# A two-layer hybrid backbone: input loaded and normed first, turned vectors in one PSUM bank, context modulated last

## The chip, the cores and the metric

The kernel runs on one core of a Trainium2 chip. The metric is the device time of one execution in microseconds (us); of several runs the median is taken. One profiled execution gives the trace that is read here. In the trace PE is TensorE's matrix multiplication, PEld its weight load, DVE VectorE, ACT ScalarE, POOL GpSimd, and SP the engine whose queue issues most of the transfers (DMA) from memory.

## What is computed

Two layers work on a latent stream `x` of 512 tokens by 1024 channels; a context of 256 tokens takes part in the first one. Each layer norms its input, scales and shifts it by vectors that are products of a conditioning vector with a weight matrix, mixes tokens, and adds the gated result to the stream. Everything is float32. What matters here is the front of layer 0:

```
def _ada(cvec, w, b):
    m = jax.nn.silu(cvec) @ w + b
    return jnp.split(m, 3, axis=-1)          # shift, scale, gate

def _modulate(x, g, shift, scale):
    return _rmsnorm(x, g) * (1 + scale) + shift

...
shift, scale, gate = _ada(c, ada_w[i], ada_b[i])
h = _modulate(x, norm_g[i], shift[:, None], scale[:, None])
shift_c, scale_c, gate_c = _ada(c_ctx, ada_w[i], ada_b[i])
hc = _modulate(ctx, norm_g[i], shift_c, scale_c)
...
p = h @ w_in                                  # q, v, forward and backward forget, gate
```

Both `h` and `hc` are then multiplied by the same 1024 by 10240 matrix `w_in`, and a gated linear recurrence runs over the results, in 16 heads. Layer 1 is a convolution module. Neither the recurrence nor layer 1 is touched by the change.

## The kernel before

Channels lie on the 128 partitions, in eight blocks (`k` = 0 to 7); tokens run along the free dimension. Every float32 factor of a large product is split into two parts, `hi` (rounded by ScalarE) and `lo` (the remainder, by VectorE or GpSimd), and a product of `[128 x 128]` weights with 512 tokens is three matrix instructions: hi by hi, hi by lo, lo by hi.

The front of the program, inside the pool `pinit` (`pi`), has these pieces:

- The **conditioning products** come in four parts, `jj` = 0 to 3, each with four 512 KB tiles `ada`. `ada_start(jj)` multiplies them (L147, 16 instructions into the PSUM tile `adaps`), copies the result to SBUF (L149, `adarow`), turns it from a row into columns by four small products (L152, into a PSUM tile `adat`, a new one for each `jj`), and adds biases (L155, L156: `mod_s`, `mod_g`). `adaps`, `adat` and the sums of squares share the pool `ps_m`, which has two buffers under the tag `ms`.
- The **input** `x_sb` (2 MB, four loads) is squared and summed (`rms_rstd`: ACT L178, DVE or POOL L180, a product with ones at L186, then ACT L187 and L188). Part `jj` gives the scales of the channel blocks 2jj and 2jj+1: each is multiplied by the norm (L254, `xn`), scaled and shifted (`modulate`: ACT L192 writes `h_hi`, DVE L193 and L194 write `h_lo`).
- **Early products**: five weight pieces (`we`, 512 KB each; three in loop turn 0, two in turn 1) are loaded, split (L136, L138) and multiplied with each pair of blocks as soon as it stands (L243 to L245, PSUM tiles `pe`): 5 x 8 x 3 = 120 matrix instructions.
- The **context** `c_sb` (1 MB, two loads) is normed likewise (`rc`), multiplied by its norm on POOL (L266) and modulated into `hc`, tiles of 256 tokens. `CTX_AT` = 2 places its loads and norm in turn 2; `CTX_MOD` places six blocks of its modulation in turn 2 and two in turn 3.

Then `pinit` closes and the pool `pt` takes its memory. The first instructions that write into `pt` (ACT L580, which takes the finished early products out of PSUM into `sg`, and DVE L313) wait for the last use of the memory below them. The products with the context (`pc`, L293 to L296) follow on TensorE; they need a PSUM buffer that L580 frees. From there on eight groups of heads go through the recurrence.

Each engine executes its instructions in the order of its own queue. That order comes from a scheduler, which works with its own model of times when the kernel is built, except that the loads issued by `load` keep the order of the code among themselves. Tile names carry a running number in the listings below; `mod_s`, `mod_g`, `xn`, `h_lo`, `hc` and `c_sb` are as above.

Of the kernel before, what the change touches and what calls it, by code (L numbers as in the profile page):

```python
# [16 lines left out]
P = 128  # L17
# [18 lines left out]
EARLY, EARLY_LOADS, CTX_AT = 5, (3, 2, 0, 0), 2  # L36
RX_BUFS, RX_ENG, WE_ENG = 3, (0, 0, 1, 0, 0, 1, 0, 0), (1, 1, 0, 0, 0)
CTX_MOD = ((), (), (0, 1, 2, 3, 4, 5), (6, 7))
# [22 lines left out]
def hybrid_kernel(ctx: ExitStack, tc: tile.TileContext, xT, ctxT, cvec, consts, norm_g, ada_b, ada_a, ada_c,  # L61
# [79 lines left out]
    def ada_start(jj, raws, pool, scz, sel):  # L141

        ps = ps_m.tile([P, 512], F32, name=f"adaps{jj}", tag="ms")
        for kk, raw in enumerate(raws):
            for k in range(2):
                c = (2 * kk + k) % 4
                mm(ps[32 * c:32 * (c + 1)], lhsT=scz[:, 2 * kk + k, :], rhs=raw[:, k, :], start=(kk < 2), stop=(kk >= 2))  # L147
        row = pool.tile([P, 512], F32, name=f"adarow{jj}", tag="adarow", bufs=2)
        V.tensor_copy(out=row, in_=ps)  # L149
        pt_ = ps_m.tile([P, 512], F32, name=f"adat{jj}", tag="ms")  # L150
        for i in range(4):
            mm(pt_[:, 2 * i:2 * i + 2], lhsT=row[:, i * P:(i + 1) * P], rhs=sel, start=True, stop=True)  # L152
        for i in range(2):
            j = 2 * jj + i
            V.tensor_scalar(out=mod_s[:, j, :], in0=pt_[:, 2 * i:2 * i + 2], scalar1=ab[:, 0, j:j + 1], scalar2=None, op0=ALU.add)  # L155
            V.tensor_scalar(out=mod_g[:, j, :], in0=pt_[:, 4 + 2 * i:6 + 2 * i], scalar1=ab1[:, j:j + 1],  # L156
                            scalar2=ng[:, 0, j:j + 1], op0=ALU.add, op1=ALU.mult)

# [43 lines left out]
    with l0:  # L202
# [8 lines left out]
        with tc.tile_pool(name="pinit", bufs=1) as pi:  # L211
# [9 lines left out]
            for jj in range(4):  # L221
                araws.append([pi.tile([P, 2, 512], F32, name=f"ada{jj}_{kk}", tag="araw", bufs=8) for kk in range(4)])
                for kk in range(4):
                    load(araws[jj][kk], ada_a[jj, kk])
                if jj == 0:
                    for i in range(4):
                        load(x_sb[:, 2 * i:2 * i + 2, :], xT[:, 2 * i:2 * i + 2, :])
                for i in todo[:EARLY_LOADS[jj]]:
                    wraws.append(wpool.tile([P, KD, P], F32, name=f"we{i}_raw", tag="raw"))
                    load(wraws[i], wsrc[i])  # L230
# [7 lines left out]
            early, done = [], {}  # L238
# [9 lines left out]
            for jj in range(4):  # L248
                ada_start(jj, araws[jj], pi, scz, sel)
                if jj == 0:  # L250
                    rs = rms_rstd([x_sb[:, k, :] for k in range(KD)], L, pi, ps_m, "rx", RX_ENG)
                for k in (2 * jj, 2 * jj + 1):
# [715 lines left out]
```

## Time and profile before

| | |
|---|---|
| median of 3 runs | 1325.85 us (1321.75 to 1326.63) |
| the profiled execution | 1325.56 us, of which the span from the first to the last instruction is 1323.5 us |
| PE busy | 1288.8 us, 97% of the span |
| DVE, ACT, POOL busy | 934.4, 608.2, 304.3 us |
| chain that ended last, by engine | PE 77%, DVE 13%, ACT 4%, DMA 3%, waits for issue 2%, POOL 1% |
| mean granted TensorE clock | 0.991 |
| first product with the context | 69.89 us after the start |

TensorE is busy nearly throughout. The first of the page's 40 slices (33 us each) is the one in which it is least busy (6 tenths) and the transfers are most (9 tenths, 352 GB/s). The change touches only what lies ahead of 70 us.

### The profile page before, as it was taken

How to read it: one execution, taken by the hardware profiler on the slowest of the kernel's cores; microseconds unless marked ns; L12 is line 12 of the kernel's file. 1: busy time of each engine (PE TensorE's matmuls, PEld its weight loads, DVE VectorE, ACT ScalarE, POOL GpSimd, SP SyncE). 2: the span in 40 equal slices, each digit the busy share in tenths (PEclk: the TensorE clock that was granted, in tenths of full speed). 3: DMA queues.
4: the chain of work that ended last, by engine and by line, in shares of the span. 5: the costliest groups of instructions: out<-in, count | busy, mean ns of one | idle time of the engine just before them, and what ended most of it. 6: DMA issues, size and time to landing. Idle time of an engine off the chain costs nothing.

```text
span 1323.5 us, 19786 instructions
## 1 busy us (share of the span) xinstructions
PE 1288.8 (97%) x7956; PEld 1087.4 (82%) x7956; DVE 934.4 (71%) x1513; ACT 608.2 (46%) x920; POOL 304.3 (23%) x289
## 2 busy tenths in 40 slices
PE   6999999999999999999999999999999999999997
PEld 2698898888889888889889889876877778788887
DVE  6667987796787888687689788865666576574233
ACT  4355564552464354565256455524423233385331
POOL 2231330330231151151024033104212112112121
PEclk8999999999999999999999999999999999999999
DMA  9322113114112312213311311213433333123321
GB/s 352 156 80 79 51 49 128 49 49 159 54 47 77 128 49 77 84 49 97 112 36 62 122 39 48 75 48 108 135 103 122 120 96 119 64 80 96 96 80 64
DMA packets 36188, 120.22 MB, mean 91 GB/s; under 512 B 4643, under 2 KB 7107, under 8 KB 36097
## 3 DMA queue, kind: packets, MB, share of 16 engines
q1 hardware_dynamic: 35104, 115.79, 26.0%
q0 software_dynamic: 992, 3.18, 1.1%
q8 instruction: 62, 1.02, 0.3%
q14 instruction: 30, 0.24, 0.1%
HBM read 116.85 MB, written 2.10 MB: 90 GB/s over the span
## 4 chain that ended last, share of the span: by engine, by line
PE 77%; DVE 13%; ACT 4%; DMA 3%; issue 2%; POOL 1%; SPq 0%; DVEq 0%; ACTq 0%
PE pa L734 4%; PE pa L735 4%; PE pa L739 4%; PE pz L293 3%; PE pz L294 3%; PE pz L296 3%; PE op L563 2%; PE cop L876 2%; PE cop L880 2%; PE op L565 2%; PE op L564 2%; PE cop L877 2%; PE pgt L803 2%; PE pgt L801 2%; PE pgt L800 2%; PE py L773 2%
## 5 line engine op out<-in xcount | busy, mean ns | idle before, releaser
L734 PE MATMUL pa<-ci_hi,h_hi 128*128 128x512 f32 x256 | 100.3, 403 | 1.9 <-ACT h_hi L682 1.9
L735 PE MATMUL pa<-ci_lo,h_hi 128*128 128x512 f32 x256 | 99.7, 393 | 0.0
L293 PE MATMUL pz<-h_hi,wz_hi 128*128 128x512 f32 x232 | 92.1, 397 | 1.4 <-ACT wz_hi L136 1.4
L294 PE MATMUL pz<-h_lo,wz_hi 128*128 128x512 f32 x232 | 91.7, 395 | 0.0
L116 POOL TENSOR_SCALAR sg<-sg 128x1536 f32<-128x1536 f32 x16 | 75.6, 4726 | 63.6 <-ACT sg L582 63.3
L167 DVE SCALAR_TENSOR_TENSOR adacc<-adb,sc,adacc 128x128 f32<-128x128 f32 x224 | 76.9, 357 | 3.8
L424 DVE SCALAR_TENSOR_TENSOR h_S<-h_S,h_dec,h_kb 128x128 f32<-128x128 f32 x96 | 59.0, 614 | 27.1 <-ACT h_kb L418 26.0
L136 ACT ACTIVATE ci_hi<-ci_raw 128x1024 fp32r<-128x1024 f32 x29 | 30.8, 1061 | 102.2 <-PE pa L739 57.9
L138 POOL TENSOR_TENSOR ci_lo<-ci_raw,ci_hi 128x1024 fp32r<-128x1024 f32 x18 | 44.2, 2461 | 129.2 <-ACT ci_hi L136 102.9
L739 PE MATMUL pa<-ci_hi,h_lo 128*128 128x512 f32 x224 | 70.9, 392 | 0.0
L510 POOL TENSOR_TENSOR h_A<-a,a 128x512 f32<-128x512 f32 x16 | 36.6, 2290 | 129.8 <-DVE a L491 108.0
L304 PE MATMUL pv<-wv_hi,h_hi 128*128 128x256 f32 x256 | 63.3, 284 | 0.0
L305 PE MATMUL pv<-wv_hi,h_lo 128*128 128x256 f32 x256 | 63.3, 284 | 0.0
L296 PE MATMUL pz<-h_hi,wz_lo 128*128 128x512 f32 x232 | 60.7, 396 | 0.0
L734 PEld LDWEIGHTS pa<-ci_hi,h_hi 128*128 128x128 f32 x256 | 48.7, 190 | 14.1 <-issue 4.1
L136 ACT ACTIVATE wz_hi<-wz_raw 128x1024 fp32r<-128x1024 f32 x29 | 30.7, 1057 | 63.6 <-DMA wz_raw<-in_w_in 54.7
L294 PE MATMUL pc<-hc,wz_hi 128*128 128x256 f32 x232 | 59.1, 288 | 0.0
L293 PE MATMUL pc<-hc,wz_hi 128*128 128x256 f32 x232 | 58.8, 287 | 0.0
L735 PEld LDWEIGHTS pa<-ci_lo,h_hi 128*128 128x128 f32 x256 | 48.7, 190 | 11.5 <-issue 1.4
L138 DVE TENSOR_TENSOR wz_lo<-wz_raw,wz_hi 128x1024 fp32r<-128x1024 f32 x29 | 35.5, 1223 | 31.1 <-ACT wz_hi L136 30.7
L876 PE MATMUL cop<-zhi,co_hi 128*128 128x512 f32 (+1 forms) x160 | 54.2, 352 | 0.0
L369 POOL TENSOR_TENSOR h_ref<-h_tot,h_gt 128x64 f32<-128x64 f32 x16 | 16.8, 1048 | 160.5 <-DVE h_ref L396 157.3
(332 smaller groups left out, 3862.1 us busy)
## 6 DMA issues: line engine op xcount, KB each, us to landing
adb<-in_ada_c SPq DMA_DIRECT2D x32, 512.0 KB, 3.2
ci_raw<-in_c_in SPq DMA_DIRECT2D x32, 512.0 KB, 3.2
wz_raw<-in_w_in SPq DMA_DIRECT2D x29, 512.0 KB, 3.2
ada<-in_ada_a SPq DMA_DIRECT2D x16, 512.0 KB, 10.2
wv_raw<-in_w_v SPq DMA_DIRECT2D x16, 512.0 KB, 3.2
wg_raw<-in_w_in SPq DMA_DIRECT2D x16, 512.0 KB, 3.2
cg_raw<-in_c_gate SPq DMA_DIRECT2D x16, 512.0 KB, 3.2
co_raw<-in_c_out SPq DMA_DIRECT2D x16, 512.0 KB, 3.6
```

The costliest lines, as they stand in the source:

```text
L116: (G if pool_min else V).tensor_scalar(out=t, in0=t, scalar1=EMAX, scalar2=None, op0=ALU.min)
L138: lo_eng.tensor_tensor(out=lo, in0=raw, in1=hi.bitcast(F32), op=ALU.subtract)
L167: V.scalar_tensor_tensor(out=acc, in0=raw[:, k, :], scalar=sc[:, k, 0:1], in1=acc, op0=ALU.mult, op1=ALU.add)
L293: mm(ps[:, :T], lhsT=hi[:, k, :], rhs=rhi[k], start=(k == 0), stop=False)
L294: mm(ps[:, :T], lhsT=hi[:, k, :], rhs=rlo[k], start=False, stop=False)
L296: mm(ps[:, :T], lhsT=lo[:, k, :], rhs=rhi[k], start=False, stop=(k == KD - 1))
L304: mm(ps[:, :256], lhsT=lhi[k][:, c], rhs=hi[:, k % 4, :], start=(k == 0), stop=False)
L305: mm(ps[:, :256], lhsT=llo[k][:, c], rhs=hi[:, k % 4, :], start=False, stop=False)
L734: mm(pss[t], lhsT=h_hi[:, 2 * kq + k, c], rhs=hi[:, k, :], start=(kq == 0 and k == 0), stop=False)
L735: mm(pss[t], lhsT=h_hi[:, 2 * kq + k, c], rhs=lo[:, k, :], start=False, stop=False)
L739: mm(pss[t], lhsT=h_lo[:, 2 * kq + k, c], rhs=hi[:, k, :], start=False, stop=(kq == 3 and k == 1))
L876: mm(ps, lhsT=hi[:, i, c], rhs=zhi[ct][:, tok], start=(ct == 0), stop=False)
```

## The change

It does three things. The four loads of `x_sb` go ahead of the `ada` tiles of part 0, and the norm of the input (`rms_rstd`) stands ahead of `ada_start(0)` in the code. The turned vectors of all four parts go into one PSUM tile, `adat`, in the bank of the pool `ps_o`, each part with eight columns of it; the conditioning products of a part are issued after the last turning product of the part before. And the context is loaded and normed in turn 3 (`CTX_AT` = 3), with all eight blocks of its modulation there too.

```
-EARLY, EARLY_LOADS, CTX_AT = 5, (3, 2, 0, 0), 2
+EARLY, EARLY_LOADS, CTX_AT = 5, (3, 2, 0, 0), 3
-CTX_MOD = ((), (), (0, 1, 2, 3, 4, 5), (6, 7))
+CTX_MOD = ((), (), (), tuple(range(KD)))
...
-    def ada_start(jj, raws, pool, scz, sel):
+    def ada_start(jj, raws, pool, scz, sel, adat, last):
...
-                mm(ps[32 * c:32 * (c + 1)], lhsT=scz[:, 2 * kk + k, :], rhs=raw[:, k, :], start=(kk < 2), stop=(kk >= 2))
+                with tc.issue_after(last.ins) if last else nullcontext():
+                    mm(ps[32 * c:32 * (c + 1)], lhsT=scz[:, 2 * kk + k, :], rhs=raw[:, k, :], start=(kk < 2), stop=(kk >= 2))
...
-        pt_ = ps_m.tile([P, 512], F32, name=f"adat{jj}", tag="ms")
+        pt_ = cut(adat, 8 * jj, [[1, 8]])
         for i in range(4):
-            mm(pt_[:, 2 * i:2 * i + 2], lhsT=row[:, i * P:(i + 1) * P], rhs=sel, start=True, stop=True)
+            last = mm(pt_[:, 2 * i:2 * i + 2], lhsT=row[:, i * P:(i + 1) * P], rhs=sel, start=True, stop=True)
...
+        return last
...
-                for kk in range(4):
-                    load(araws[jj][kk], ada_a[jj, kk])
                 if jj == 0:
                     for i in range(4):
                         load(x_sb[:, 2 * i:2 * i + 2, :], xT[:, 2 * i:2 * i + 2, :])
+                for kk in range(4):
+                    load(araws[jj][kk], ada_a[jj, kk])
...
+            adat = ps_o.tile([P, 512], F32, name="adat", tag="o")
...
-                ada_start(jj, araws[jj], pi, scz, sel)
                 if jj == 0:
                     rs = rms_rstd([x_sb[:, k, :] for k in range(KD)], L, pi, ps_m, "rx", RX_ENG)
+                turned = ada_start(jj, araws[jj], pi, scz, sel, adat, turned)
```

The scheduler orders the queues anew, but only in this front part: behind it every engine's queue holds the same instructions in the same order. Three places show what moved (lines from L142 on stand one to three lower in the changed kernel).

VectorE at the first pair of channel blocks, before: the vectors of part 0 (`mod_s`, `mod_g`), then the rest of the input's squares, a weight split, and the multiplications by the norm.

```order
L149 COPY adarow_191<-adaps_182 128x512
L180 TENSOR_TENSOR rx_sq_202<-rx_sq_202,rx_sq_204 128x512
L155 TENSOR_SCALAR mod_s<-adat_193,ab 128x2
L156 TENSOR_SCALAR mod_g<-adat_193,ab_108,ng 128x2
...
L180 TENSOR_TENSOR rx_sq_202<-rx_sq_202,rx_sq_221 128x512
L138 TENSOR_TENSOR we_lo<-we_raw,we_hi 128x1024
L254 TENSOR_TENSOR xn_229<-x_sb,rx_sq_202 128x512
```

The same place now:

```order
L182 TENSOR_TENSOR rx_sq_183<-rx_sq_183,rx_sq_202 128x512
L257 TENSOR_TENSOR xn_229<-x_sb,rx_sq_183 128x512
...
L257 TENSOR_TENSOR xn_278<-x_sb,rx_sq_183 128x512
L150 COPY adarow_219<-adaps_210 128x512
L138 TENSOR_TENSOR we_lo<-we_raw,we_hi 128x1024
L156 TENSOR_SCALAR mod_s<-adat,ab 128x2
L157 TENSOR_SCALAR mod_g<-adat,ab_108,ng 128x2
```

The multiplications by the norm went ahead of the weight split, and the vectors of part 0 went behind it.

TensorE at the context's sum of squares (`rc_ss`), before: behind the turning of part 2 and ahead of the conditioning products of part 3.

```order
L245 MATMUL pe_293<-h_hi,we_lo 128x512
L152 MATMUL adat_335<-sel,adarow_333 128x2 x4
L186 MATMUL rc_ss<-rc_sq_384,ones 128x256
L147 MATMUL adaps_435<-ada_0_172,scz 32x512 x2
L147 MATMUL adaps_435<-ada_1_173,scz 32x512 x2
```

The same product now:

```order
L248 MATMUL pe_292<-h_hi,we_lo 128x512
L153 MATMUL adat<-sel,adarow_391 128x2 x4
L188 MATMUL rc_ss<-rc_sq_441,ones 128x256
L246 MATMUL pe_243<-h_hi,we_hi 128x512
L246 MATMUL pe_248<-h_hi,we_hi 128x512
```

It went behind the turning of part 3, the last one, and so behind 30 more early products; the conditioning products of part 3 (`adaps`) now stand ahead of all this.

VectorE at the last vectors (part 3) and the context, before: six blocks of the context stand ahead of `mod_s` and `mod_g` of part 3, two among the last blocks of the input.

```order
L193 TENSOR_SCALAR c_sb<-c_sb,mod_g,mod_s 128x256 x2
L194 TENSOR_TENSOR hc_114<-c_sb,hc_112 128x256
L155 TENSOR_SCALAR mod_s<-adat_446,ab 128x2
L156 TENSOR_SCALAR mod_g<-adat_446,ab_108,ng 128x2
L194 TENSOR_TENSOR hc_114<-c_sb,hc_112 128x256
...
L193 TENSOR_SCALAR xn_460<-xn_460,mod_g,mod_s 128x512
L193 TENSOR_SCALAR c_sb<-c_sb,mod_g,mod_s 128x256
L194 TENSOR_TENSOR h_lo<-xn_460,h_hi 128x512
L194 TENSOR_TENSOR hc_114<-c_sb,hc_112 128x256
L313 TENSOR_SCALAR qs_0_696<-pe_288 128x512
```

The same place now:

```order
L157 TENSOR_SCALAR mod_g<-adat,ab_108,ng 128x2
L195 TENSOR_SCALAR xn_401<-xn_401,mod_g,mod_s 128x512
L196 TENSOR_TENSOR h_lo<-xn_401,h_hi 128x512
L195 TENSOR_SCALAR xn_406<-xn_406,mod_g,mod_s 128x512
L196 TENSOR_TENSOR h_lo<-xn_406,h_hi 128x512
L195 TENSOR_SCALAR c_sb<-c_sb,mod_g,mod_s 128x256
L196 TENSOR_TENSOR hc_113<-c_sb,hc_111 128x256
...
L195 TENSOR_SCALAR c_sb<-c_sb,mod_g,mod_s 128x256 x2
L196 TENSOR_TENSOR hc_114<-c_sb,hc_112 128x256 x2
L316 TENSOR_SCALAR qs_0_693<-pe_287 128x512
```

All 16 context instructions of VectorE now stand behind the input's last block, directly ahead of the first instruction in the new pool. On the queue of SP the two context loads went from ahead of the `ada` tiles of part 3 to behind them, and two weight loads for later stages (`wz_11`, `wv_0`) went in among those tiles.

## Rows read from the trace of the kernel before

**Rows 1.** Windows: stretch in us, its length, each engine's busy us, PEclk, DMA share, GB/s.
```profile
24.00:46.00 22.00, 20.67 (x88) 12.42 (x89) 15.91 (x36) 8.25 (x16) 0.00 (x0) 1.00 0.98 378
...
58.00:60.00 2.00, 0.01 (x1) 0.01 (x1) 1.76 (x9) 0.88 (x2) 0.00 (x0) 1.00 0.00 0
60.00:69.20 9.20, 9.04 (x30) 6.64 (x30) 3.54 (x9) 1.63 (x3) 0.00 (x0) 0.81 0.01 2
...
70.00:110.00 40.00, 40.00 (x289) 37.88 (x290) 30.64 (x47) 25.43 (x38) 14.81 (x12) 1.00 0.24 80
```

**Rows 2.** Timeline to 34 us: start, us, engine, line, tiles [idle before <-releaser].
```profile
17.36 4.75 POOL L138 TENSOR_TENSOR we_lo<-we_raw,we_hi 128x1024 fp32r<-128x1024 f32 x2 [1.12 <-ACT we_hi L136]
...
18.77 1.06 ACT L136 ACTIVATE we_hi<-we_raw 128x1024 fp32r<-128x1024 f32 x1 [0.21 <-DMA we_raw<-in_w_in]
...
19.86 3.33 DVE L138 TENSOR_TENSOR we_lo<-we_raw,we_hi 128x1024 fp32r<-128x1024 f32 x1 [2.28 <-ACT we_hi L136]
...
21.84 0.63 ACT L188 ACTIVATE rx_sq<-rx_sq 128x512 f32<-128x512 f32 x1
...
23.12 2.48 DVE L254 TENSOR_TENSOR xn<-x_sb,rx_sq 128x512 f32<-128x512 f32 x4
...
23.84 1.52 ACT L192 ACTIVATE h_hi<-xn,mod_s,mod_g 128x512 fp32r<-128x512 f32 x2 [1.36 <-DVE xn L254]
...
27.28 0.50 PE L244 MATMUL pe<-h_lo,we_hi 128*128 128x512 f32 x1 [0.63 <-DVE h_lo L194]
...
33.89 1.34 ACT L178 ACTIVATE rc_sq<-c_sb 128x256 f32<-128x256 f32 x4
```

**Rows 3.** Chain that ended last, 41 to 48 us: start, us it adds, engine, line.
```profile
41.50 0.24 PE pe L244
41.74 0.98 PE adaps L147 x4
42.72 0.43 PE pe L244
...
46.39 0.80 PE adat L152 x8
```

**Rows 4.** Timeline from the turning of part 2 to the context's multiplication.
```profile
47.03 0.68 PE L186 MATMUL rc_ss<-rc_sq,ones 128*128 128x256 f32 x2
47.21 0.22 DVE L155 TENSOR_SCALAR mod_s<-adat,ab 128x2 f32<-128x2 f32 x1 [2.89 <-PE adat L152]
...
47.65 0.81 ACT L192 ACTIVATE h_hi<-xn,mod_s,mod_g 128x512 fp32r<-128x512 f32 x1 [8.86 <-DVE mod_g L156]
...
47.99 1.92 PE L147 MATMUL adaps<-ada,scz 128*32 128x512 f32 x16 [0.28 <-DVE mod_g L156]
...
49.44 0.41 ACT L188 ACTIVATE rc_sq<-rc_sq 128x256 f32<-128x256 f32 x1
...
49.92 7.05 POOL L266 TENSOR_TENSOR c_sb<-c_sb,rc_sq 128x256 f32<-128x256 f32 x8 [27.81 <-ACT rc_sq L188]
```

**Rows 5.** Timeline of the context's modulation and of the end of the front.
```profile
52.30 1.57 DVE L193 TENSOR_SCALAR c_sb<-c_sb,mod_g,mod_s 128x256 f32<-128x256 f32 x2
...
57.04 0.75 DVE L194 TENSOR_TENSOR hc<-c_sb,hc 128x256 fp32r<-128x256 f32 x2
...
59.12 0.81 ACT L192 ACTIVATE h_hi<-xn,mod_s,mod_g 128x512 fp32r<-128x512 f32 x1 [3.16 <-DVE mod_g L156]
...
69.24 1.58 ACT L580 ACTIVATE sg<-pe 128x512 f32<-128x512 f32 x3 [7.61 <-PE pe L245]
```

**Rows 6.** Lines L193 and L194, 45 to 70 us: times in ns, least/median/most.
```profile
L193 DVE TENSOR_SCALAR c_sb<-c_sb,mod_g,mod_s x8: 403/620/830, 52.3 to 62.2; 128x256 f32<-128x256 f32 x8
L193 DVE TENSOR_SCALAR xn<-xn,mod_g,mod_s x4: 542/545/547, 48.5 to 61.7; 128x512 f32<-128x512 f32 x4
...
L194 DVE TENSOR_TENSOR hc<-c_sb,hc x8: 413/416/957, 53.8 to 63.1; 128x256 fp32r<-128x256 f32 x8
L194 DVE TENSOR_TENSOR h_lo<-xn,h_hi x4: 677/686/693, 49.1 to 62.5; 128x512 fp32r<-128x512 f32 x4
```

More of the change, by code (lines that the diff above doesn't have):

```diff
@@ L237, in hybrid_kernel @@
             load(mk, consts[:, C_MASK:C_FWD].rearrange("p (a b) -> p a b", a=5))
-            early, done = [], {}
+            early, done, turned = [], {}, None
+            adat = ps_o.tile([P, 512], F32, name="adat", tag="o")
             def early_products(upto):
```

## The prediction

> **What bounds the kernel now.** The page's table of engines has TensorE busy for 97% of the span, and its 40 slices show the one soft place at the beginning. From 70 us on TensorE is busy 40.00 us of 40 [rows 1], so only the end of the front can move: the instant at which ScalarE may take the early products out of PSUM (L580) and the new pool opens. That is 69.24 us now, released by TensorE [rows 5]. What the change does to the whole is therefore the new instant less 69.24, plus any difference in TensorE's clock just behind it. The queues behind the front hold the same instructions in the same order, so nothing else can move.
>
> Inside the front I read the windows next. From 24 to 46 us TensorE is busy 20.67 us of 22 while the transfers take 98% of their engines: both are near full. [...]
>
> **The change part by part.** *Input first.* The norm of the input stands at 21.84 + 0.63 = 22.5 us now [rows 2]. Four pieces of 512 KB move from ahead of it to behind it; at 378 GB/s [rows 1] a piece takes 1.39 us, so the norm comes about 5.5 us sooner, near 17. But the first `h_hi` also needs part 0's vectors, and VectorE's queue now has these behind the split of the third weight piece. That piece keeps its place in the loads (ScalarE splits it at 18.77, released by the transfer), and VectorE's half runs from 19.86 to 23.19, beside GpSimd's own splits that last to 22.11 [rows 2]. From there `h_hi` follows as it does after 47.21, by 0.44 us [rows 4]: 23.6 us, against 23.84 now [rows 2]. Of 5.5 us, 0.2 is left. The split is late next.
>
> Then `h_hi` (0.81, [rows 4]), 0.55 and 0.69 us on VectorE [rows 6] make `h_lo` ready at 25.7. TensorE gets to it after three first products and one piece of conditioning products of part 1. Such a piece alone among early products takes 0.98 us and makes the next product 0.2 us longer [rows 3]: 1.18. With 24.4 + 0.7 + 1.18 TensorE's dense run begins at 26.3, against 27.28 [rows 2], but one more such piece, which is done by then now, lies in it: nothing is gained.
>
> *A bank of their own for the turned vectors.* Part 3's conditioning products wait now until part 2's vectors are read (released by `mod_g`, [rows 4]), since both use the two buffers of `ms`. With that gone they stand earlier, and part 2's run as one block. TensorE's queue from 26.3 us to the end of part 3's turning: early products of six channel blocks, 5 x 3 x 6 = 90, less the three already done, 87 at 0.233 [rows 3], 20.3 us; three lone pieces at 1.18, 3.5; part 2 in one block, 1.92 [rows 4] + 0.2; half of part 3 likewise, 1.2; three turnings at 0.80 [rows 3], 2.4. Sum 29.5, so 55.8 us. Waits inside (two weight splits of the second turn, vectors of parts 1 and 2) cost between nothing and some 1.5 us by my ordering of the queues; I take none, since each finds other products ahead of it. The ordering by `issue_after` costs nothing: TensorE executes in order anyway.
>
> *Context last.* The context's sum of squares, in the queue right behind part 2's turning now, stands behind part 3's. From the end of the turning (46.39 + 0.80 = 47.19, [rows 3]) to GpSimd's first multiplication (49.92, [rows 4]) is 2.73 us, and the same instructions lie between: 58.5. GpSimd takes 7.05 us for its eight [rows 4]: 65.6. VectorE does the input's last two blocks first (57.1 + 2 x 1.24 = 59.6) and finds the first context block ready near 60.0 (0.88 us of GpSimd, an eighth of 7.05, and ScalarE's step, taken as 0.6, three quarters of the 0.81 for a block twice as wide). It has 16 instructions. While GpSimd runs beside it, six of them took from 52.30 to 57.04, 0.79 us each; then two took 0.75 [rows 5], 0.37 each. So seven until 65.6, nine more in 3.3: 68.9. The new pool opens at **69.0 us against 69.24**.
>
> TensorE's last 30 products (57.1 + 7.0 = 64.1, or up to 65.9 with the clock loss of today) are no longer what ends last: today's idle time ahead of them goes, and a new one opens behind them, 3 to 5 us instead of 0.7. The first instruction in the new pool needs the memory below it, so it waits for VectorE's last context block, and ScalarE, GpSimd and, through the PSUM buffer, TensorE stand behind it.
>
> *Clock.* After 2.0 us without work it stayed low for 3.5 us [rows 1]. An idle stretch twice as long now lies ahead of the context products. Nothing to 3 us may be lost there; I take 1.7, what the nearest stretch lost.
>
> *Loads.* The context lands six pieces later, 33.89 [rows 2] + 6 x 1.39 = 42 us, and is first needed on TensorE at 55.8: hidden, with ten microseconds to spare for its squares. On SP's queue `wv_0` waits for a weight split, and behind it stand part 3's last tile, the context and two constants; TensorE wants that tile near 48 us, and all would have to be ten microseconds late to cost anything.
>
> **Sum.** 1325.56 (profiled execution, 2.06 of it outside the span) - 0.2 + 1.7 = 1327.1. The median of the runs before is 0.3 above that execution, within their spread; I give **1327**.
>
> **Rivals.** *VectorE and GpSimd take strict turns (slower).* Place: the context's modulation, now the last thing in the front. If every one of VectorE's 16 steps took the longest that one took beside GpSimd, 0.83 and 0.96 us [rows 6], they would need 14.3 us from 60.0: 74.3, and 1325.56 + 5.1 + 1.7 = 1332.4. It decides from a mean of 0.58 us a step on, at which the front ends later than now; 0.9 is needed for over 0.5%. For it: all steps early in the stretch are near these values. Against: GpSimd is done at 65.6, and six steps side by side averaged 0.79.
>
> [...]
>
> *TensorE's own end decides (faster).* If the context were ready by 64 us, the pool would open at 64.2 with no idle time behind: 1325.56 - 5.0 = 1320.5. For it: the context lands 13 us before it is used. Against: its sum of squares stands behind part 3's turning in an in-order queue, so GpSimd cannot start before about 58. A weaker form, lone pieces as cheap as in a block (0.48 instead of 1.18), takes 2 us off and gives 1325.
>
> [...]
>
> *It does nothing at all.* The input's norm comes sooner and nobody uses it; this is part of the forecast above and not a case apart.
>
> **How the numbers follow.** Forecast 0.66 (1324 to 1330), early clock 0.15, strict turns 0.10, TensorE's end 0.09. Beyond 0.5% (6.6 us, about what a measurement of this kernel can tell from no change) lie 1319.2 and 1332.5. Strict turns just reach the upper one, with some weight from two losses coming together: slower 0.09. TensorE's end stops 1.3 us short of the lower one, and the runs before spread by 5 us: faster 0.06. No change 0.85. The range goes from 1321, the faster rival with the spread, to 1332, the slower one.
>
> **What would show it.** Right: L583 (today's L580) starts within 2 us of 69 and is released by VectorE's last `hc`; TensorE idles 3 us or more ahead of the context products, with a clock of 0.5 behind; `h_hi` starts near 23.6; the last turning ends near 56; GpSimd's context work begins near 58.5. Wrong: a release by TensorE (the faster rival), context steps of 0.9 us to the end (the slower one), matrix instructions of 0.6 us between 26 and 30 us (early clock), or a difference behind 110 us, which nothing here explains.

## The result, and the profile after

The changed kernel takes **1332.98 us** (median of 6 runs, 1331.71 to 1335.06) against 1325.84 of the kernel before on the same chip: the ratio is 1.0054, with a 95% interval of 1.0042 to 1.0066. It is slower by 7.1 us, where 1327 with a range to 1332 was forecast. The profiled execution takes 1333.46 us with a span of 1331.4, 7.9 more than before. The functions that the diff touches stand 1 to 3 lines lower in the changed kernel (L254 is now L257, L580 is L583).

The beginning, from the timeline (start, us, engine, line, tiles, idle before and releaser); it answers [rows 2]:

```profile
16.61 0.63 ACT L190 ACTIVATE rx_sq<-rx_sq 128x512 f32<-128x512 f32 x1
17.27 6.80 DVE L257 TENSOR_TENSOR xn<-x_sb,rx_sq 128x512 f32<-128x512 f32 x4 [5.25 <-ACT rx_sq L190]
18.26 5.26 POOL L138 TENSOR_TENSOR we_lo<-we_raw,we_hi 128x1024 fp32r<-128x1024 f32 x2 [7.59 <-ACT we_hi L136]
23.99 0.68 DVE L150 COPY adarow<-adaps 128x512 f32<-128x512 f32 x1
24.59 1.21 DVE L138 TENSOR_TENSOR we_lo<-we_raw,we_hi 128x1024 fp32r<-128x1024 f32 x1
...
24.72 1.87 PE L153 MATMUL adat<-sel,adarow 128*128 128x2 f32 x8 [6.18 <-DVE adarow L150]
...
27.07 1.52 ACT L194 ACTIVATE h_hi<-xn,mod_s,mod_g 128x512 fp32r<-128x512 f32 x2 [6.99 <-DVE mod_g L157]
...
31.52 0.49 PE L247 MATMUL pe<-h_lo,we_hi 128*128 128x512 f32 x1
```

The norm is there at 17.24, as wanted. But the four multiplications by it, 2.48 us before, take 6.80, most of it beside GpSimd's weight splits (`we_lo`). The view of line L257 by itself says which of its eight are slow (ns, least/median/most):

```profile
L257 DVE TENSOR_TENSOR xn<-x_sb,rx_sq x8: 678/688/2842, 17.3 to 45.5; 128x512 f32<-128x512 f32 x8
```

The row that copies the turned vectors (`adarow`) stands behind these four in VectorE's queue, TensorE waits 6.18 us for it, the first `h_hi` comes at 27.07 instead of 23.84, and the dense run of early products begins at 31.52 instead of 27.28. The end of the front, answering [rows 4, 5]:

```profile
60.18 0.95 PE L153 MATMUL adat<-sel,adarow 128*128 128x2 f32 x8
...
63.88 6.80 POOL L269 TENSOR_TENSOR c_sb<-c_sb,rc_sq 128x256 f32<-128x256 f32 x8 [40.35 <-ACT rc_sq L190]
...
74.08 1.57 ACT L583 ACTIVATE sg<-pe 128x512 f32<-128x512 f32 x3 [2.77 <-DVE hc L196]
...
74.73 0.58 PE L296 MATMUL pc<-hc,we_hi 128*128 128x256 f32 x1 [4.88 <-ACT sg L583]
```

and the windows (stretch, length, busy us of PE, PEld, DVE, ACT, POOL, PEclk, DMA share, GB/s), answering [rows 1]:

```profile
20.00:24.00 4.00, 0.00 (x0) 0.00 (x0) 4.00 (x3) 0.08 (x1) 3.52 (x2) 0.62 1.03 370
24.00:28.00 4.00, 3.28 (x16) 1.98 (x16) 2.60 (x8) 0.93 (x2) 0.00 (x0) 0.50 0.33 89
28.00:32.00 4.00, 4.00 (x13) 1.46 (x10) 3.93 (x9) 1.60 (x3) 0.00 (x0) 0.60 0.98 374
69.00:72.00 3.00, 0.85 (x4) 0.37 (x2) 3.00 (x7) 1.80 (x3) 1.67 (x3) 1.00 0.00 0
72.00:76.00 4.00, 1.27 (x6) 1.27 (x7) 3.21 (x8) 1.92 (x4) 0.16 (x3) 0.52 0.01 2
76.00:80.00 4.00, 4.00 (x24) 4.00 (x24) 0.20 (x1) 3.17 (x6) 0.00 (x0) 0.63 0.00 0
```

The pool opens at 74.08, 4.84 us later than before, released by VectorE's last `hc`. TensorE waits 4.88 us in all, to 74.73, and then runs at a granted clock of 0.51 from 74.7 to 79.0 us and of 1.00 from there to 80 us. A third place lies outside the front. Behind 110 us the view of waits has one that is 2.8 us long and was 1.0 us before:

```profile
PE h_pp L420 <- ACT h_kb L417: 2.8, 1, 2.8
```

The same wait before:

```profile
PE h_pp L417 <- ACT h_kb L414: 1.0, 1, 1.0
```

ScalarE's step on `h_kb` stands behind the rounding of a weight piece (`wz_hi`, L136), and that piece came late. Its load was issued at 130.70 and rounded at 135.93, 5.23 us later; before, 124.10 and 127.48, 3.38 us. These are the SyncE issue and the ScalarE step, before:

```profile
124.10 0.33 SPq L198 DMA_DIRECT2D wz_raw<-in_w_in  x1
127.48 1.06 ACT L136 ACTIVATE wz_hi<-wz_raw 128x1024 fp32r<-128x1024 f32 x1 [3.16 <-DMA wz_raw<-in_w_in]
```

And in the changed kernel, with the DMA queues in the tenth of a microsecond from 131.7 (packets, MB, time as a share of 16 engines):

```profile
130.70 0.33 SPq L200 DMA_DIRECT2D wz_raw<-in_w_in  x1
135.93 1.06 ACT L136 ACTIVATE wz_hi<-wz_raw 128x1024 fp32r<-128x1024 f32 x1 [5.00 <-DMA wz_raw<-in_w_in]
```

```profile
q8 instruction: 1, 0.02, 126.2%
```

q8 carries packets of the kind "instruction": 62 over the run, 1.02 MB, so 16 KB each. This one takes 1.26 x 16 x 0.1 = 2.0 us of one DMA engine and begins 1.1 us behind the weight load's issue.

The account in the traces, as differences to before at four instants: the pool opens +4.84; the weight piece that was rounded at 116.28 is rounded +6.60; the first sum of L544 (154.7) +8.4; the span +7.9. So the front gives 4.84, the half clock behind it 1.8, the late load 1.8, and 0.5 comes back, net, in the rest (between 885 and 915 us; see **Open** below).

### The profile page after: what moved, and what is told of

Its sections match the earlier page's. It is cut to its first block, busy times and chain, and to the rows that moved or that the text cites. A ratio compares the mean times of both kernels' runs of the same rounds, so it can differ in the third digit from the quotient of the medians.

```text
span 1331.4 us, 19780 instructions
## 1 busy us (share of the span) xinstructions
PE 1285.9 (97%) x7956; PEld 1087.7 (82%) x7956; DVE 937.7 (70%) x1513; ACT 608.0 (46%) x920; POOL 304.1 (23%) x289
## 3 DMA queue, kind: packets, MB, share of 16 engines
q8 instruction: 62, 1.02, 0.3%
## 4 chain that ended last, share of the span: by engine, by line
PE 74%; DVE 13%; ACT 3%; DMA 2%; issue 1%; POOL 1%; DVEq 0%; ACTq 0%
PE pa L737 4%; PE pa L738 4%; PE pa L742 4%; PE pz L296 3%; PE pz L297 3%; PE pz L299 3%; PE op L566 2%; PE cop L879 2%; PE cop L883 2%; PE cop L880 2%; PE op L568 2%; PE op L567 2%; PE pgt L806 2%; PE pgt L804 2%; PE pgt L803 2%; PE py L776 2%
## 5 line engine op out<-in xcount | busy, mean ns | idle before, releaser
L136 ACT ACTIVATE ci_hi<-ci_raw 128x1024 fp32r<-128x1024 f32 x29 | 30.8, 1060 | 102.2 <-PE pa L742 58.0
L136 ACT ACTIVATE wz_hi<-wz_raw 128x1024 fp32r<-128x1024 f32 x29 | 30.7, 1057 | 68.6 <-DMA wz_raw<-in_w_in 55.0
```

## The experiments

Three theories were put to runs. **A**: the start costs the time, since the norm's multiplications now lie beside GpSimd's weight splits. **B**: the tail costs it, since the context is modulated last, with TensorE idle and slow behind. **C**, formed on the first four traces: an instruction packet that meets a weight load near 130 us costs it. The recorded expectations call such a packet a code load.

All the traces by those instants and the first early product with `h_lo` ("first lo product"), as differences to before from the third column to the span. The runs of one kernel spread by 2 to 8 us and a trace is one of them: that of input_only is its fastest run, that of norm_from_psum its slowest. The ratios rest on all runs, each against the kernel before on the same chip (medians 1325.57 to 1326.87).

| kernel | first lo product | pool opens | piece of 116.28 | sum of 154.7 | span | median us | ratio, 95% |
|---|---|---|---|---|---|---|---|
| before | 27.28 | 69.24 | 116.28 | 154.7 | 1323.5 | 1325.84 | |
| after | 31.52 | +4.84 | +6.60 | +8.4 | +7.9 | 1332.98 | 1.0054, 1.0042 to 1.0066 |
| input_only | 32.08 | +5.47 | +5.40 | +5.3 | +3.5 | 1332.38 | 1.0043, 1.0031 to 1.0056 |
| bank_only | 27.21 | -1.72 | -1.79 | +1.2 | +0.3 | 1325.76 | 0.9997, 0.9987 to 1.0008 |
| input_back | 26.91 | +0.62 | +2.37 | +5.2 | +5.0 | 1328.86 | 1.0022, 1.0013 to 1.0031 |
| ctx_back | 31.25 | +4.60 | +4.66 | +8.2 | +6.1 | 1333.55 | 1.0053, 1.0041 to 1.0066 |
| splits_on_vector | 26.39 | -1.77 | -0.94 | +3.8 | +3.5 | 1329.27 | 1.0025, 1.0016 to 1.0034 |
| norm_from_psum | 28.30 | +1.98 | +4.00 | +8.8 | +8.6 | 1332.24 | 1.0046, 1.0030 to 1.0061 |
| keep_busy | 31.36 | +4.71 | +4.00 | +5.2 | +5.2 | 1330.76 | 1.0036, 1.0024 to 1.0048 |
| code_shift | 26.70 | -0.71 | -0.60 | +0.5 | +0.6 | 1326.15 | 1.0005, 0.9996 to 1.0013 |
| three_products | 26.32 | -1.21 | -1.22 | -0.8 | -3.5 | 1324.14 | 0.9983, 0.9974 to 0.9991 |
| x_ahead_of_ctx | 27.07 | -4.51 | -4.52 | -1.2 | -1.8 | 1322.15 | 0.9973, 0.9964 to 0.9982 |
| all_three_mended | 27.97 | -3.88 | -3.88 | -2.0 | -2.4 | 1322.71 | 0.9972, 0.9961 to 0.9984 |
| x_ahead_three | 27.09 | -4.47 | -4.38 | -4.3 | -5.7 | 1320.29 | 0.9951, 0.9936 to 0.9966 |

### The three parts taken apart

input_only: of the diff, the loads and the norm ahead of `ada_start`, and nothing else (the moved loads are left out here).

```diff
...
-                ada_start(jj, araws[jj], pi, scz, sel)
                 if jj == 0:
                     rs = rms_rstd([x_sb[:, k, :] for k in range(KD)], L, pi, ps_m, "rx", RX_ENG)
+                ada_start(jj, araws[jj], pi, scz, sel)
```

> The kernel before with the first part alone: the input is loaded and its norm formed ahead of the first conditioning products; the turned vectors stay in the rotating PSUM tiles, the context stays in turn 2. Theory A (the start: VectorE's first four multiplications by the norm run beside GpSimd's two weight splits and take 6.8 us instead of 2.5, so the modulated input comes at 27 us and the dense run of products starts 4.2 us late at half clock): the four multiplications take over 5 us, the first lo product is at 31 to 32 us against 27.3 before, and the kernel takes 1329 to 1331. Theory B (the tail: context modulated last leaves TensorE idle and at half clock behind the last turning): nothing of that is here, so the time is 1325 to 1327.

bank_only: the bank and the `issue_after`, with loads, norm and context as before. Of its differences to the kernel before:

```diff
...
-        pt_ = ps_m.tile([P, 512], F32, name=f"adat{jj}", tag="ms")
+        pt_ = cut(adat, 8 * jj, [[1, 8]])
...
```

> The kernel before with the second part alone: the turned vectors in a PSUM bank of their own, with conditioning products issued behind the turning before them; input and context as before. Both theories expect the first lo product near 27.3 us as before and a time of 1324 to 1327; a time over 1328 would say that the bank or the strict order of the turnings costs something, which neither theory holds.

input_back: the changed kernel, with the `ada` tiles of part 0 loaded ahead of `x_sb` again (left out here) and the conditioning products ahead of the norm again.

```diff
...
+                turned = ada_start(jj, araws[jj], pi, scz, sel, adat, turned)
                 if jj == 0:
                     rs = rms_rstd([x_sb[:, k, :] for k in range(KD)], L, pi, ps_m, "rx", RX_ENG)
-                turned = ada_start(jj, araws[jj], pi, scz, sel, adat, turned)
```

> The changed kernel without its first part: conditioning products ahead of the input's norm again, bank and context-last kept. Theory A: the first lo product is back at 27 to 28 us, the last turning ends near 56 to 57 instead of 61.1, the pool behind the front opens at 69 to 70 instead of 74.1, and the time is 1327 to 1329 (only the half clock behind the front is left). Theory B: the tail is what costs, so most of the 7.1 us stays: 1331 to 1333.

ctx_back: the changed kernel with the two constants of before.

```diff
-EARLY, EARLY_LOADS, CTX_AT = 5, (3, 2, 0, 0), 3
+EARLY, EARLY_LOADS, CTX_AT = 5, (3, 2, 0, 0), 2
-CTX_MOD = ((), (), (), tuple(range(KD)))
+CTX_MOD = ((), (), (0, 1, 2, 3, 4, 5), (6, 7))
```

> The changed kernel with its context put back into turn 2 (six modulations there, two in turn 3), input-first and the bank kept. Theory A: the four multiplications still take over 5 us and the first lo product is still at 31 to 32 us, so 1329 to 1332 stays. Theory B: with the tail gone the time is back at 1325 to 1327.

The input part alone costs nearly as much as the whole change (+6.8 us at the median; its five runs give a ratio of 1.0031 to 1.0056, which is 4.1 to 7.4 us), the bank nothing, and the whole change without its input part +3.2. In the traces of input_only and ctx_back the four multiplications again take 6.79 and 6.81 us. The context's place costs 3.1 us where the input is as before (input_back against bank_only, 1328.86 and 1325.76) and nothing where the input comes first (1332.98 against 1333.55 of ctx_back). Theory B alone falls; A carries most. The sizes expected under A held for input_back (1327 to 1329), and bank_only came out as expected. They were missed in the other two: input_only and ctx_back came out 1.4 and 1.6 us above A's range. For ctx_back the trace says where: +4.66 at 116 us has become +8.2 at 155. And bank_only, which opens its pool 1.72 us early, is 1.2 us late at 155. So something behind the front, other than the context, gives time away too.

### Why the four multiplications take 6.8 us

splits_on_vector: the changed kernel with one constant different, so that GpSimd splits no weights.

```diff
-RX_BUFS, RX_ENG, WE_ENG = 3, (0, 0, 1, 0, 0, 1, 0, 0), (1, 1, 0, 0, 0)
+RX_BUFS, RX_ENG, WE_ENG = 3, (0, 0, 1, 0, 0, 1, 0, 0), (0, 0, 0, 0, 0)
```

> The changed kernel with the first two weight splits on VectorE instead of GpSimd, so that GpSimd does nothing beside the four multiplications by the norm. If it is GpSimd's work beside them that stretches the four from 2.5 to 6.8 us (theory A), they take 2.5 to 2.8 us here, the modulated input comes near 24.4 instead of 27.1 us (VectorE then has three splits of 1.2 us of its own ahead of the turned vectors' additions), the first lo product near 28 to 29 instead of 31.5, and the time is 1329 to 1331. If the four are slow for another reason (the loads that run at full rate in that stretch, or the tiles' places), they stay over 5 us, and the kernel is slower than the changed one by the splits' 2.4 us: 1335 or more.

norm_from_psum: the changed kernel, with the norm also written to PSUM, and read from there by the first four.

```diff
...
+        if name == "rx":
+            act(out=ps[:, :T], in_=acc[0], func=AF.Exp, scale=-0.5)
         act(out=acc[0], in_=acc[0], func=AF.Exp, scale=-0.5)
...
-                    V.tensor_tensor(out=t, in0=x_sb[:, k, :], in1=rs, op=ALU.mult)
+                    V.tensor_tensor(out=t, in0=x_sb[:, k, :], in1=rs[1 if k < 4 else 0], op=ALU.mult)
```

> The changed kernel, with ScalarE writing the input's norm a second time into the PSUM tile of its sums, and VectorE's first four multiplications reading it from there; GpSimd's two splits run beside them as in the changed kernel. If two operands read from SBUF beside GpSimd's two are what clash, the four take 2.5 to 3.5 us and GpSimd's splits about 4.8 us, the modulated input comes at 23.5 to 24 us and the time is 1328 to 1330; if any VectorE work is slowed beside GpSimd's, they stay over 5 us and the time is 1333 to 1334.

The four of splits_on_vector, its first `h_hi` and its first lo product, from the timeline, and the window from 24 us:

```profile
16.80 2.50 DVE L257 TENSOR_TENSOR xn<-x_sb,rx_sq 128x512 f32<-128x512 f32 x4 [5.26 <-ACT rx_sq L190]
...
23.65 1.52 ACT L194 ACTIVATE h_hi<-xn,mod_s,mod_g 128x512 fp32r<-128x512 f32 x2 [4.05 <-DVE mod_g L157]
...
26.39 0.50 PE L247 MATMUL pe<-h_lo,we_hi 128*128 128x512 f32 x1
```

```profile
24.00:28.00 4.00, 3.96 (x16) 1.99 (x15) 3.47 (x8) 2.36 (x4) 0.00 (x0) 1.00 0.90 278
```

and of norm_from_psum, with GpSimd's splits beside them:

```profile
16.86 2.48 DVE L259 TENSOR_TENSOR xn<-x_sb,rx_ss 128x512 f32<-128x512 f32 x4 [5.23 <-ACT rx_ss L191]
17.88 4.68 POOL L138 TENSOR_TENSOR we_lo<-we_raw,we_hi 128x1024 fp32r<-128x1024 f32 x2 [7.59 <-ACT we_hi L136]
...
24.00 1.52 ACT L196 ACTIVATE h_hi<-xn,mod_s,mod_g 128x512 fp32r<-128x512 f32 x2 [3.78 <-DVE mod_g L157]
```

Without GpSimd the four take 2.50 us; with GpSimd, but one operand from PSUM, 2.48, and GpSimd keeps its 4.68. The loads ran at full rate in both (DMA share 1.03). So the four are slow where VectorE reads two operands from SBUF beside GpSimd's splits, 6.80 us against 2.48 with one of them in PSUM: the rivals named beforehand (the loads, the tiles' places, any VectorE work beside GpSimd's) would have kept the four over 5 us in one run or the other.

splits_on_vector opens its pool 6.6 us earlier than the changed kernel and wins 3.7 of them (1329.27, within the 1329 to 1331 that were expected); 4.7 us go between 116 and 155 us, where the changed kernel loses 1.8. norm_from_psum opens 2.9 us earlier than the changed kernel, and its median stays at 1332.24 (runs from 1327.49 to 1334.18), against the 1328 to 1330 that were expected. In its trace, its slowest run, `h_hi` comes at 24.00 as expected, but TensorE still runs at 0.50 from 24 to 28 us, after a wait of 2.8 us for that `h_hi`, and 4.8 us are lost between 116 and 155.

### The half clock behind the front

keep_busy: the changed kernel with products that nothing reads (`early_products` now returns its last one).

```diff
...
-            early_products(KD)
+            end = early_products(KD)
+            for i in range(40):
+                with tc.issue_after(end.ins):
+                    mm(adat[:, 256:512], lhsT=early[0][0][0][:, 0, :], rhs=h_hi[:, 0, 0:256], start=True, stop=True)
```

> The changed kernel with 40 products that nothing reads behind the last early product (128x256 each, some 4.8 us at full clock), which fill the hole in which TensorE waits for the context's last lo part and falls to half clock. The clock in 72 to 80 us stays 1.00 instead of 0.52 and 0.63, the first context tile takes 2.9 instead of 4.8 us, so 1.9 us are gained there: 1330.5 to 1331.5 if that half clock is a cost of its own; unchanged if what follows waits for something else. The 80 more TensorE instructions also move the place of its later code loads; if the wait of TensorE for ScalarE near 133 us (2.8 us against 1.0 before) comes from the code load that lies beside a weight load at 131 us, that wait goes too, and the time falls by up to 1.8 more.

Windows of keep_busy (busy us of PE, PEclk, DMA share, GB/s):

```profile
72.00:76.00 4.00, 3.87 (x32) 1.00 0.01 2
76.00:80.00 4.00, 4.00 (x36) 1.00 0.00 0
```

The pool opens as late as in the changed kernel, 73.95 against 74.08, but the clock stays at 1.00, and the first weight piece `wg` is rounded at 91.43 us instead of 93.30: 1.9 us are won there, far ahead of the late load. The kernel takes 1330.76, 2.2 us less and within the 1330.5 to 1331.5 that were expected. So the half clock behind the front is a cost of its own, which products that do nothing avoid. As expected, the wait on `h_kb` is 1.1 us here instead of 2.8; the weight piece ahead of that one is late in its place (4.49 us behind its issue).

### The instruction packet and the weight load

code_shift: bank_only, with products at the very beginning.

```diff
...
             adat = ps_o.tile([P, 512], F32, name="adat", tag="o")
+            for i in range(20):
+                mm(adat[:, 64 + i:65 + i], lhsT=ones, rhs=ones[:, 0:1], start=True, stop=True)
```

> The kernel with the bank alone, and 20 one-column products ahead of all others, where TensorE waits for the first loads anyway: they move every later code load of TensorE by 40 instructions and cost nothing at their place. The bank alone opened the pool behind the front 1.7 us earlier than the kernel before (67.5 against 69.2) and lost that near 127 us, where ScalarE waited 4.6 us for a weight load (3.2 before) and TensorE 2.4 us for ScalarE (1.0 before), with a code load of TensorE beside that weight load. Theory C (the code load delays the last packets of the weight load): with the code load moved, the wait is back at 1.0 us and the time is 1323.5 to 1324.5. Otherwise (the shift of 1.7 us itself, or the place of the tiles, makes the load late): the wait stays at 2.4 us and the time at 1325.8.

three_products: the kernel before, with three of them.

```diff
             early, done = [], {}
+            spare = ps_o.tile([P, 512], F32, name="spare", tag="o")
+            for i in range(3):
+                mm(spare[:, i:i + 1], lhsT=ones, rhs=ones[:, 0:1], start=True, stop=True)
```

> The kernel before, with nothing moved: three one-column products that nothing reads are put ahead of all others on TensorE, into the PSUM bank that the change uses for its turned vectors. They cost nothing at their place, and move every later code load of TensorE earlier by a few instructions. In the kernel before, the code load near 127 us begins 2.80 us after the weight load beside it is issued, when that load is all but done (ScalarE waits 3.2 us, TensorE 1.0 us); in six kernels with the bank it began 1.0 to 2.64 us after the issue, and the weight load came 1.3 to 2.0 us later. Theory C (the place of the code load): here it begins under 2.7 us after the issue, ScalarE waits over 4.4 us, TensorE 2.3 us or more and then runs at half clock for a while, and the kernel takes 1327 to 1330. Rival (the bank's place, or the shift of the work itself): 1325 to 1326.5, with the wait at 1.0 us.

Neither time came out as theory C had it. In code_shift the wait on `h_kb` is back at 1.0 us, as expected, but the instruction packet now meets the load before (rounded 4.49 us behind its issue), the pool opens 1.0 us later than with the bank alone, and the time is 1326.15 instead of 1323.5 to 1324.5. three_products was expected slower and is faster by 2.3 us: the packet moved 2.4 us ahead, to 0.4 us behind the load's issue, which theory C in its first form held to be a costly place, and costs little there (3.80 us). Its gain lies elsewhere. 1.2 us are in the front, 0.9 of them already at 8.9 us, when the last `ada` piece of part 0 is multiplied (9.8 before); 2.7 come between 885 and 915 us, where the granted clock is 0.79 from 884 to 892 and from 904 to 912 in the trace of before and 1.00 in both here. All traces together, for the load of this place that the packet comes nearest to (in keep_busy and code_shift the one ahead of the others'; begins by the packet's own start, up to 0.1 us more than the recorded texts have it, which go by tenths):

| kernel | packet begins behind the issue, us | piece rounded behind the issue, us |
|---|---|---|
| three_products, x_ahead_three | 0.4, 0.4 | 3.80, 3.50 |
| after, code_shift | 1.1, 1.1 | 5.23, 4.49 |
| all_three_mended, ctx_back, norm_from_psum | 1.7 each | 5.14, 5.37, 5.33 |
| splits_on_vector, x_ahead_of_ctx | 1.9, 2.2 | 5.41, 5.31 |
| keep_busy, input_back, bank_only | 2.3, 2.5, 2.7 | 4.49, 4.65, 4.86 |
| input_only, before | 2.8, 2.9 | 3.34, 3.38 |

Where the packet begins 1.1 to 2.7 us behind the issue, the piece comes 1.1 to 2.0 us later than the 3.38 of before, in ten traces of ten; in the other four it comes 0.4 us later at most. These bounds were drawn from the first traces; x_ahead_three below is the one run that was put to them beforehand. The other loads of the same traces bear them out: 512 KB weight loads land 3.2 us behind their issue at the median, and behind 100 us, over all 14 traces, the 22 with a packet that begins 1.0 to 2.25 us behind the issue, and no other near, land after 4.2 to 5.8 us, every one. In bank_only the clock then falls to 0.66 between 130 and 135 us (1.00 before), and the two together cost it 3.0 us by 155.

Whose instructions the packets carry is read from two things: adding products to TensorE's queue moves them (three products by 2.4 us, in three_products), and where the kernel before, with TensorE's 7956 products and as many weight loads, has 62 packets, keep_busy, with 40 products more, has 63. So they are taken here as TensorE's. How a packet delays a load is not shown: no row has the order in which a DMA engine serves the two.

### A version that beats both

The bank alone leaves one thing to win: part 3's vectors are turned at 55.1 us, and VectorE, busy with the context, takes them at 58.2. x_ahead_of_ctx puts them and the last two input blocks first, and keeps the context's norm, with GpSimd's multiplications, in turn 2. Against bank_only:

```diff
...
+N_FREE = 2
-CTX_MOD = ((), (), (0, 1, 2, 3, 4, 5), (6, 7))
+CTX_MOD = ((), (), (), tuple(range(KD)))
...
-    def modulate(t, k, gcol, scol, hi, lo):
+    def modulate(t, k, gcol, scol, hi, lo, last=None):
         act(out=hi[k], in_=t, func=AF.Identity, scale=gcol, bias=scol)
-        V.tensor_scalar(out=t, in0=t, scalar1=gcol, scalar2=scol, op0=ALU.mult, op1=ALU.add)
+        with tc.issue_after(last.ins) if last else nullcontext():
+            V.tensor_scalar(out=t, in0=t, scalar1=gcol, scalar2=scol, op0=ALU.mult, op1=ALU.add)
...
+                    for k in range(KD):
+                        G.tensor_tensor(out=c_sb[:, k, :], in0=c_sb[:, k, :], in1=rc, op=ALU.mult)
                 for k in CTX_MOD[jj]:
-                    G.tensor_tensor(out=c_sb[:, k, :], in0=c_sb[:, k, :], in1=rc, op=ALU.mult)
-                    modulate(c_sb[:, k, :], k, mod_g[:, k, 1:2], mod_s[:, k, 1:2], hc_hi, hc_lo)
+                    modulate(c_sb[:, k, :], k, mod_g[:, k, 1:2], mod_s[:, k, 1:2], hc_hi, hc_lo, mod if jj == 3 and k >= N_FREE else None)
```

(`mod` is the last input block's `h_lo` step.)

> The bank alone, and on VectorE the last part's vectors and input steps ahead of six of the eight context columns (context still normed in turn 2, GpSimd's eight multiplications at 50 to 57 us as before). In the bank alone the turned vectors of part 3 are there at 55.1 us and VectorE takes them at 58.2, behind context steps; TensorE waits 2.3 us for that. Theory (order on VectorE, not the place of the load, is what the context's move should have changed): vectors at 55.5, TensorE's early products end near 64.7 instead of 67, VectorE's twelve context steps run behind them with GpSimd idle, 0.42 us each, to 64.5, and the pool opens at 64.5 to 65.5 against 69.2 of the kernel before; 1321 to 1324 at the end. Rival (the context becomes last, as in the changed kernel): the pool opens at 67 or later and the time is 1325 or more.

all_three_mended adds the input first, with all splits on VectorE, to it.

> All three parts with their costs taken out: the input normed first with all weight splits on VectorE (no GpSimd beside the multiplications), the bank, and the context normed in turn 2 with six of its columns behind the last input steps on VectorE. From the splits-on-VectorE run: the first lo product at 26.4 us against 27.3 before, early products dense from there; TensorE's early products end near 63 to 64 and the pool opens at 63.5 to 65. Theory A and B together: 1320 to 1323. If the context still comes last, the pool opens at 66 to 67.5 with TensorE idle ahead of it: 1324 to 1329.

x_ahead_three is x_ahead_of_ctx with three one-column products in the bank, as in code_shift.

> The kernel with the input steps ahead of the context on VectorE, and the three one-column products ahead of all others. In twelve traces so far the third weight load of in_w_in behind 110 us is taken by ScalarE 3.3 to 3.4 us after its issue where TensorE's code load begins 2.7 us or more behind the issue, 3.8 us where it begins 0.4 us behind it, and 4.5 to 5.4 us where it begins between 1.0 and 2.6 us behind it; in the kernel without the three products it began 2.15 us behind it, the load was taken after 5.3 us, TensorE waited 3.0 us and ran at half clock behind that, and 3.4 of the 4.5 us that the front had gained were gone by 142 us. Theory C: if the code load now begins outside 0.4 to 2.7 us behind the issue, the load is taken within 3.8 us, TensorE waits under 1.5 us there, over 3 us of the front's gain are kept at 142 us, and the time is 1319 to 1321; if it still begins inside, nothing changes: 1322. A load that is late although the code load lies outside, or early although it lies inside, speaks against theory C.

x_ahead_of_ctx, from the timeline (its lines stand 2 to 3 lower again):

```profile
56.41 0.82 ACT L195 ACTIVATE h_hi<-xn,mod_s,mod_g 128x512 fp32r<-128x512 f32 x1 [0.88 <-DVE mod_g L158]
...
59.65 2.02 DVE L197 TENSOR_SCALAR c_sb<-c_sb,mod_g,mod_s 128x256 f32<-128x256 f32 x6
...
61.58 2.10 DVE L198 TENSOR_TENSOR hc<-c_sb,hc 128x256 fp32r<-128x256 f32 x6
...
64.73 1.58 ACT L586 ACTIVATE sg<-pe 128x512 f32<-128x512 f32 x3 [5.82 <-PE pe L250]
```

With GpSimd done, twelve context steps take 4.0 us, 0.34 each, while TensorE's last products run, and TensorE opens the pool at 64.73. Pool and time (1322.15) are as expected. Of the 4.5 us, 3.3 are lost by 155 us: the load is late, and the granted clock behind it is 0.67 from 125 to 130 us. Its load, and that of x_ahead_three with its packet:

```profile
119.65 0.33 SPq L202 DMA_DIRECT2D wz_raw<-in_w_in  x1
124.96 1.06 ACT L137 ACTIVATE wz_hi<-wz_raw 128x1024 fp32r<-128x1024 f32 x1 [5.08 <-DMA wz_raw<-in_w_in]
```

```profile
119.69 0.33 SPq L202 DMA_DIRECT2D wz_raw<-in_w_in  x1
123.19 1.06 ACT L137 ACTIVATE wz_hi<-wz_raw 128x1024 fp32r<-128x1024 f32 x1 [3.27 <-DMA wz_raw<-in_w_in]
```

x_ahead_three issues the load at the same instant and has its piece 1.8 us sooner, its packet begins at 120.1, 0.4 us behind the issue instead of 2.2, the clock is 1.00 from 125 to 130 us, and 4.3 of 4.5 us are still there at 155. All this was expected of theory C, though the packet lies right at the edge that was named for it, 0.4. It takes **1320.29 us**, 0.9951 of the kernel before (0.9936 to 0.9966), against 0.9973 (0.9964 to 0.9982): in the times the two intervals just touch, so that the gain rests on the traces as well. all_three_mended opens 0.6 us later than x_ahead_of_ctx (TensorE at 0.53 and 0.62 from 20 to 28 us) and takes the same time, within what was expected, though the first lo product was expected at 26.4 and came at 27.97: with its contention out, the input's place neither wins nor loses anything that shows.

## Why the prediction was wrong

**The step that failed** is the first one, "VectorE's half runs from 19.86 to 23.19 ... From there `h_hi` follows": 23.6 against 27.07. The split isn't what is late. With the norm at 17.24, VectorE's queue has the four multiplications first, and the prediction has no term for them: at 2.48 us as before they would be done ahead of the split, at nothing. At their new place they lie beside GpSimd's splits and cost 4.3 us more (6.80 against 2.48), and everything for `h_hi` waits behind them; 3.5 us of it reach `h_hi`. splits_on_vector shows that this is the step, and not the chain behind it: with the four at 2.50 us `h_hi` comes at 23.65 and the dense run begins at 26.39, where the forecast had 23.6 and 26.3. [rows 2] had the sign of it: the split of 128x1024 took 3.33 us beside GpSimd, and a later one, alone, in the same trace 1.22:

```profile
29.85 1.22 DVE L138 TENSOR_TENSOR we_lo<-we_raw,we_hi 128x1024 fp32r<-128x1024 f32 x1
```

That ratio of 2.7 on 2.48 us gives 6.8, an estimate from the rows of before alone. What VectorE and GpSimd cost each other was weighed for the context (0.79 us a step beside GpSimd and 0.37 alone, from [rows 5]), and not for the start.

**The dense run** was to begin 2.7 us behind `h_hi` and began 4.45 behind it. The early clock, given 0.15 among the chances, is a dense run that begins at a low granted clock, and so it came: TensorE did nothing from 20 to 24 us, and the clock was 0.50 from 24 to 28 (forecast from [rows 1]: 1.00). It cost 4.45 - 2.7 = 1.75 us. The runs bear it out: from `h_hi` to the dense run it is 2.74 us in splits_on_vector, at a clock of 1.00 from 24 to 28 us, and 4.30 in norm_from_psum, at 0.50 there. The two together are 31.52 - 26.3 = 5.2 us, and they go through to the opening of the pool.

**What held.** TensorE's queue from the dense run to the last turning: 29.5 us, measured 29.6 (31.52 to 61.13). From there to GpSimd's context work: 2.73, measured 2.75. From GpSimd's start to VectorE's last context step: 10.4, measured 10.0 (to 73.92), so "strict turns" is out: the 16 steps follow each other at 0.53 us on average (8.5 us from the first to the last one's end), where that rival was to decide from 0.58 on. The pool released by `hc`, 3 us or more without work on TensorE: 4.88. The clock loss behind it: 1.7, measured 1.8, and shown by keep_busy. The pool would have opened at 69.0 + 5.2 = 74.2; it opened at 74.08.

The 1.7 comes from the stretch of before that [rows 1] has at 0.81: 0.19 of 9.2 us is 1.75 us. The stretch in four windows (busy us of PE, PEclk, DMA share, GB/s):

```profile
60.00:62.00 2.00, 1.89 (x6) 0.88 0.00 0
62.00:64.00 2.00, 2.00 (x6) 0.50 0.00 0
64.00:66.00 2.00, 2.00 (x9) 0.77 0.04 8
66.00:69.20 3.20, 3.15 (x14) 1.00 0.00 0
```

The first three lose 0.24, 1.00 and 0.46 us, 1.7 in all; at 0.50 that is 3.4 us, where the prediction has 3.5.

**"Nothing else can move"** was wrong as well. The order behind the front is the same, but by the trace 1.8 us were lost from 131 us on, behind a load that met an instruction packet, whose place among the loads the change had moved. The text named "a difference behind 110 us, which nothing here explains" as what would show it wrong. The forecast's 1327.1 with 5.1, 0.1 and 1.8 us is 1334.1; the profiled execution took 1333.46, so 0.6 came back in the rest.

**The range and the chances.** The forecast was one number with a chain of terms behind each other. Its first term was wrong by 3.5 us, and the early clock, which stood apart as a rival, came on top of it with 1.75: together as much as the whole range allowed above the forecast (5 us), ahead of the late load.

**Open.** Why three products move the packet by 2.4 us. Why the first loads are 0.9 us sooner in three_products. Where the traces differ behind 155 us, most of it lies between 885 and 915 us: the granted clock falls there twice in the trace of before and in that of norm_from_psum for longer than in the others, once in most, and not at all in three_products and ctx_back; whether the kernel or the single execution decides that isn't shown. That the late load costs the changed kernel 1.8 us is read from its trace: no run moves its packet alone. Whether the late load also decides in the runs without a profile isn't shown either: medians and traces agree in order, not in each microsecond.

## What to carry to other kernels

A step that a reordering moves has the price of its new neighbours: before it is counted as free, look which engine with SBUF operands runs beside it there, and take the slowest row that the trace has of such a pair (here 2.48 us became 6.80). Where a change leaves TensorE waiting, price the clock behind the wait as a term of its own and not as a rival: here it was 0.81 behind 2.0 us without work and 0.52 behind 4.9, though it stayed at 1.00 behind the 2.8 us to 138.2 in the changed kernel. And a change that only adds or moves instructions can shift a kernel by some 2 us through its instruction packets (1322.15 and 1320.29 for the same work): before a small loss or gain is put down to an idea, look whether one load far from the edit has become late.

## What the runs showed of the hardware

- Two SBUF operands on VectorE beside GpSimd's splits: four multiplications of 128x512 took 6.80 us, single ones up to 2.84; with one operand in PSUM the four took 2.48, and GpSimd's two splits 4.68 (5.26 in the changed kernel).
- A 16 KB instruction packet took 0.96 us of one DMA engine near the end of a load (bank_only, 60.1% of 16 x 0.1 us) and 2.0 us in the middle of one (after). Where it began 1.1 to 2.7 us behind the issue of a 512 KB weight load, that load was late by 1.1 to 2.0 us, in ten traces of ten.
- 4.9 us without work on TensorE cost 1.8 us of clock behind them (after, 0.51 from 74.7 to 79.0 us); unread products in the hole gave 2.2 us back at the median (keep_busy).
